# Attention scores in two packed passes of 128 rows and a third of 32 rows on two row groups

## Chip, core and metric

One core of a Trainium2 chip runs the whole kernel. The metric is the device time of one execution in microseconds (us). TensorE (PE) multiplies, VectorE (DVE), ScalarE (ACT) and GpSimd (POOL) work on the results, and SyncE (SP) issues most DMAs.

## What is computed

Two layers of a decoder trunk over 528 tokens (16 learned "meta" tokens and 512 others) with 1024 channels. Each layer projects the normed input, mixes one part by causal pooling and another by latent attention, gates both and adds them to the residual. The change is in the scores of the attention; 8 heads, each with 64 plain and 32 rotary dimensions:

```python
q = (c_q @ w_q_b).reshape(B, L, N_HEADS, QK_HEAD_DIM)          # 64 + 32
k = jnp.concatenate([k_nope, k_pe], axis=-1)                   # k_pe shared by the heads
q, k = rmsnorm(q, g_qn), rmsnorm(k, g_kn)                      # then rotary on the last 32
s = jnp.einsum('bqhd,bkhd->bhqk', q[:, q0:kend], k[:, :kend]) * scale
s = jnp.where(valid, s, MASK_VALUE); p = softmax(s); o = p @ v
```

## The kernel before

**Precision.** Every operand of a product is split into a rounded high part (type float32r) and a low part, the rest. A product is three matmuls into the same PSUM bank: high by high, high by low, low by high (`mm3`, L210 to L214; the big projections go through it as L211, L212, L213). A matmul has a stationary operand, loaded by a weight load of 128 columns, and a moving one.

**Scores of a head** (`head`, L825). Rows of the operands are the 96 dimensions. `qh` and `ql` (tiles `qhl`) hold the high and low part of the queries, `kh` and `kl` those of the keys. Even heads use 96 rows: 64 plain ones, then 32 rotary ones; odd heads 128, with the rotary ones at 0 and zeros at 32 to 63. For block i of 128 queries the moving operand is the keys up to its end: 144, 272, 400 and 528 columns. The last is cut at column 240 (`SPL`) into 240 and 288. So a head has five score pieces, of 272 (`s1`), 240 (`s3`), 400 (`s2`), 288 (`s4`) and 144 (`s0`) columns, three passes each; in layer 0 a sixth of 16 queries by 16 keys (`sm_`, the meta tokens). They lie in three PSUM banks, all of the pool `S` with three buffers: `sa` holds `s1` and `s3`, `sb` holds `s2`, `sc` holds `s4`, `s0` and `sm_`. `scores` (L838) writes the large pieces, `passes` (L890) those of 144 and 16 columns, which the profile shows as L891. `top` (L842, on DVE) adds the mask and takes the row's extreme, `expo` (L849, on ACT) takes the exponential (L850), and `turn` (L852) transposes on DVE and copies the meta columns on POOL.

**Operands of a head** (`prep`, L803). ACT rounds 64 rows of queries (L811), DVE takes their rest (L814), POOL copies the rotary rows of keys (L819) and queries (L821) and, for even heads, 64 rows of keys (L817). `prep` of head h + 1 is called behind `head` of head h. `rope_keys` (L566) makes the rotary keys of four heads at a time, `keys` (L795) the plain ones of two.

**What sets the order.** The program is written as a stream of projections (`stream`, L220) between whose steps the attention of a layer is laid by hand: `gap` (L1159) and `fill_now` (L303) advance the stream by so many nominal ns. On top of that a scheduler orders the instructions of every engine by the dependences and its own estimates. `follow` (L312) fixes an order between two instructions without a wait, `behind` (L316) adds a wait. On each engine instructions run in the order that results.

**Other places.** `qk_stats` (L764) takes the norms of queries and keys: `stat_go` (L530) sums squares with small matmuls (L538), `stat_rows` (L542) copies them with ACT (L546) into `srows`, a tile zeroed at the start (L163). `kr_sums` (L504) and `norm_sums` (L430) are matmuls too whose stationary operand is 32 columns wide at column positions 0, 32, 64 and 96; L538 has 16 columns at such positions. `pv` (L976) multiplies by the values with stationary operands of 128 columns (L994) and 64 (L997).

Of the kernel before, what the change touches and what calls it, by code (L numbers as in the profile page):

```python
# [43 lines left out]

C_ID, C_MASK = 0, 128
C_IK, C_IR = 256, 286
C_KPE, C_CQ = 306, 314
C_MM, C_VBD, C_INVF, C_CNT = 330, 346, 354, 355
N_CONST = 419

# [31 lines left out]
def trunk(ctx, tc, xT, xrow, mrow, pos, win, wkr, wqb, wkb, wvb, wgr, wpu, wmu, wout, gains, const, yT):  # L82
# [69 lines left out]
    posb = slot("u3", I32)  # L152
    ident = cst[:, C_ID:C_ID + P]
    ones = cp.tile([P, P], F32, name="ones")
# [6 lines left out]

    srows = cp.tile([32, T], F32, name="srows")
    gp.memset(srows, 0.0)  # L163

# [138 lines left out]
    def fill_now(ns):  # L303
        end = clk[0] + ns
        while clk[0] < end and step():
            pass
# [47 lines left out]
    class Layer:  # L354
# [187 lines left out]
        def stat_rows(self):  # L542
            t, n = srows, 2 * H
# [17 lines left out]
        def spread_rope(self, r):  # L561
            self.bcr = bc = slot("bc", bufs=3)
            for i in range(4):
                sp.dma_start(bc[32 * i:32 * i + 32], kdr[self.l][4 * r + i:4 * r + i + 1, :].partition_broadcast(32))

# [198 lines left out]
        def qk_stats(self):  # L764
            fill_now(LAG + 700)
            self.stat_go()
            self.stat_rows()
            sts = srows
            fill_now(2600)
# [33 lines left out]
        def prep(self, h):  # L803
            p, odd = h // 2, h % 2
            n0, r0 = (64, 0) if odd else (0, 64)
            kd = self.ks[p][odd]
            g0, gq = 32 * (h % 4), 32 * SEAT[h % 4]
            qh, ql = qhl[odd]
            x0 = self.x0
            src = self.qn[p][n0:n0 + 64, x0:T]  # L810
            made = act.activation(qh[n0:n0 + 64, x0:T], src, AF.Copy)  # L811
            if h == 0:
                behind(made, newest[0])
            dve.tensor_sub(ql[n0:n0 + 64, x0:T], src, qh[n0:n0 + 64, x0:T].bitcast(F32))  # L814
            if odd == 0:
                for d, f in zip(kd, self.ks[p][1]):
                    gp.tensor_copy(d[0:64, :], f[0:64, :])  # L817
            for d, f in zip(kd, self.kr[h // 4]):
                gp.tensor_copy(d[r0:r0 + 32, :], f[g0:g0 + 32, :])  # L819
            for d, f in zip((qh, ql), self.qr[h // 4]):  # L820
                gp.tensor_copy(d[r0:r0 + 32, x0:T], f[gq:gq + 32, x0:T])  # L821
            m = P if odd else QK
            return [t[0:m] for t in (*kd, qh, ql)]

        def head(self, h, kq, prev):  # L825
            kh, kl, qh, ql = kq
            odd = h % 2
# [9 lines left out]

            def scores(i, out, a, b):  # L838
                q0 = NM + P * i
                return mm3(out, qh[:, q0:q0 + P], ql[:, q0:q0 + P], kh[:, a:b], kl[:, a:b], True, True)  # L840

# [23 lines left out]
            top(1, 1, s1, causal(272))  # L865
            top(3, 4, s3, maskw[:, 0:SPL])
            sb = sct()
            s2 = sb[:, 0:400]
            scores(2, s2, 0, 400)
            top(2, 2, s2, causal(400))  # L870
# [14 lines left out]
            self.gap()  # L885
            sc = sct()
            s0, s4 = sc[:, 0:144], sc[:, 144:144 + T - SPL]
            scores(3, s4, SPL, T)

            def passes(out, q0, n):  # L890
                return [lambda k=k, q=q, x=x: pe.matmul(out, q[:, q0], x[:, 0:n], start=k == 0, stop=k == 2)  # L891
                        for k, (q, x) in enumerate(((qh, kh), (qh, kl), (ql, kh)))]

            todo = passes(s0, slice(NM, NM + P), 144)
            if not self.last:
                sm_ = sc[0:NM, 432:432 + NM]
                todo += passes(sm_, slice(0, NM), NM)
            for fn in todo:
                fn()
            if not self.last:  # L900
# [117 lines left out]
        def meta_queries(self):  # L1018
# [9 lines left out]
            dve.tensor_mul(smeta, smeta, bc(mxm))  # L1028
            tr = sm.tile([32, P], F32, tag="smt", name=nm("smt"))
            dve.transpose(tr, self.smeta32.rearrange("p a b -> p (a b)"))  # L1030
# [210 lines left out]
def constants():  # L1241
    c = np.zeros((P, N_CONST), np.float32)
    r = np.arange(P)
    c[:, C_ID:C_ID + P] = np.eye(P)
    c[:, C_MASK:C_MASK + P] = np.where(r[None, :] <= r[:, None], 0.0, NEG)
# [62 lines left out]
```

## Time and profile before

| | us |
|---|---|
| median of 3 runs | 754.3 (754.03 to 754.93) |
| profiled execution | 755.48 |
| its span in the trace | 753.7 |
| TensorE busy in the span | 748.1 |

A row of the order in time has a start, a duration, the engine (PE for matmuls, PEld for weight loads), the line, the operands (out<-in), the stationary tile as rows*columns and the moving operand as rows x columns. Matmuls are pipelined, so their durations overlap: what a matmul holds TensorE for is read from one start to the next. A row of the waits has who waited for whom, the us in total, the times and the longest. A row of a stretch has its length, then each engine's busy us with its count of instructions, the granted TensorE clock, the DMA share and GB/s.

### The profile page before, as it was taken

What the parts mean: (1) busy time and instruction counts of PE and PEld (TensorE: products, weight loads), DVE (VectorE), ACT (ScalarE), POOL (GpSimd) and SP (SyncE); (2) the same over time, 40 slices, a digit from 0 to 9 for tenths busy, and PEclk for the clock granted to TensorE, in tenths of its full rate; (3) what the DMA queues carried; (4) which work ended last, traced back from release to release, by engine and by line L of the source; (5) the groups of instructions that cost most, each with busy time, mean ns of one, the idle gap of its engine ahead of it and who ended that gap; (6) DMA issues with size and microseconds to landing.
All of it is one profiled execution on the core that took longest, in us unless ns stands there. A gap on an engine that the chain in (4) does not pass through costs nothing.

```text
span 753.7 us, 14317 instructions
## 1 busy us (share of the span) xinstructions
PE 748.1 (99%) x5010; PEld 681.9 (90%) x5010; DVE 562.3 (75%) x1214; ACT 395.2 (52%) x864; POOL 241.8 (32%) x294
## 2 busy tenths in 40 slices
PE   9999999999999999999999999999999999999998
PEld 9999899999999999999997898887788888887887
DVE  5588777658999987694367478678589999966942
ACT  6755656554656555543254456455445665554321
POOL 2126404704552520161130264038043526102400
PEclk9999999999999999999999999999999999999999
DMA  8633223434766576425643332233356666763462
GB/s 280 179 103 118 70 81 91 112 96 142 206 163 177 170 202 176 129 91 165 183 135 91 108 113 73 82 91 107 105 151 216 181 175 189 203 167 98 129 223 87
DMA packets 72798, 106.55 MB, mean 141 GB/s; under 512 B 14051, under 2 KB 34915, under 8 KB 72726
## 3 DMA queue, kind: packets, MB, share of 16 engines
q1 hardware_dynamic: 72582, 105.38, 47.8%
q8 instruction: 39, 0.64, 0.4%
q14 instruction: 33, 0.27, 0.1%
q10 hardware_dynamic: 144, 0.26, 0.1%
HBM read 89.76 MB, written 15.85 MB: 140 GB/s over the span
## 4 chain that ended last, share of the span: by engine, by line
PE 94%; DMA 4%; SPq 1%; DVE 1%; ACT 0%; issue 0%; ACTq 0%; DVEq 0%
PE mm L211 28%; PE mm L213 28%; PE mm L212 28%; PE S L211 2%; PE S L213 2%; PE S L212 2%; DMA raw<-wmu 1%; PE o L994 1%; DMA rdr<-rs 1%; PE o L997 1%; PE S L891 1%; PE S L538 1%; PE S L504 0%; DMA raw<-win 0%; DMA cq<-rdr 0%; DMA xb<-xT 0%
## 5 line engine op out<-in xcount | busy, mean ns | idle before, releaser
L213 PE MATMUL mm<-hh,wlo 128*128 128x264 f32 (+2 forms) x1072 | 337.0, 316 | 0.0
L212 PE MATMUL mm<-hl,whi 128*128 128x264 f32 (+2 forms) x1072 | 336.4, 315 | 0.0
L211 PE MATMUL mm<-hh,whi 128*128 128x264 f32 (+2 forms) x1072 | 336.3, 315 | 0.0
L207 DVE TENSOR_TENSOR wlo<-raw,whi 128x512 fp32r<-128x512 f32 (+2 forms) x239 | 179.6, 754 | 87.5 <-ACT whi L206 83.9
L206 ACT ACTIVATE whi<-raw 128x512 fp32r<-128x512 f32 (+2 forms) x239 | 143.0, 600 | 167.3 <-PE mm L212 133.2
L211 PEld LDWEIGHTS mm<-hh,whi 128*128 128x128 f32 x1072 | 201.4, 188 | 14.1 <-DVE vt L704 0.8
L212 PEld LDWEIGHTS mm<-hl,whi 128*128 128x128 f32 x1072 | 201.6, 188 | 13.0
L213 PEld LDWEIGHTS mm<-hh,wlo 128*128 128x128 f32 x1072 | 200.9, 188 | 12.3
L652 POOL TENSOR_TENSOR racc<-racc,tmp 128x264 f32<-128x264 f32 (+1 forms) x15 | 14.9, 993 | 117.7 <-ACT tmp L651 117.7
L1069 POOL TENSOR_TENSOR tmp<-tmp,xb 128x264 f32<-128x264 f32 (+1 forms) x24 | 27.7, 1166 | 41.8 <-DVE tmp L1067 39.7
L821 POOL CAST qhl<-q 32x528 fp32r<-32x528 f32 (+1 forms) x32 | 27.6, 876 | 40.5 <-PE S L891 39.1
L843 DVE CUSTOM_DVE_ANT_0 S<-S,maskw,nqs 128x240 f32<-128x240 f32 (+4 forms) x80 | 37.9, 493 | 1.5 <-PE S L213 1.3
L211 PE MATMUL mm<-cq,whi 128*128 128x264 f32 (+1 forms) x108 | 34.7, 321 | 0.0
L212 PE MATMUL mm<-th,whi 128*128 128x264 f32 (+1 forms) x108 | 34.6, 321 | 0.0
L213 PE MATMUL mm<-u,wlo 128*128 128x264 f32 (+1 forms) x108 | 34.5, 320 | 0.0
L212 PE MATMUL mm<-cq,whi 128*128 128x264 f32 (+1 forms) x108 | 34.5, 321 | 0.0
L213 PE MATMUL mm<-cq,wlo 128*128 128x264 f32 (+1 forms) x108 | 34.5, 321 | 0.0
L211 PE MATMUL mm<-u,whi 128*128 128x264 f32 (+1 forms) x108 | 34.5, 319 | 0.0
L938 POOL TENSOR_TENSOR u<-u,cq 128x512 f32<-128x512 f32 x8 | 12.9, 1616 | 64.6 <-DMA cq<-rdr 41.2
L853 POOL COPY pm<-cq 128x16 f32<-128x16 f32 x32 | 17.9, 559 | 44.4 <-ACT cq L850 42.3
L850 ACT ACTIVATE cq<-S,bia 128x400 f32<-128x400 f32 (+2 forms) x48 | 24.4, 512 | 13.9 <-DVE bia L904 12.8
L973 DVE TENSOR_TENSOR attE<-attE,th 128x640 fp32r<-128x640 f32 x32 | 25.6, 828 | 6.1 <-ACT th L972 6.1
(305 smaller groups left out, 1401.2 us busy)
## 6 DMA issues: line engine op xcount, KB each, us to landing
raw<-win SPq DMA_DIRECT2D x143, 256.0 KB, 3.5
pdr<-attD SPq DMA_DIRECT2D x16, 640.0 KB, 3.6
attE<-pdr SPq DMA_DIRECT2D x64, 160.0 KB, 3.6
raw<-wout SPq DMA_DIRECT2D x32, 256.0 KB, 3.0
raw<-wpu SPq DMA_DIRECT2D x16, 256.0 KB, 2.7
raw<-wmu SPq DMA_DIRECT2D x16, 256.0 KB, 2.7
raw<-wqb SPq DMA_DIRECT2D x12, 256.0 KB, 2.6
xb<-xT SPq DMA_DIRECT2D x8, 264.0 KB, 5.6
```

What stands on the lines that cost most here:

```text
L206: act.activation(hi[:, :n], raw[:, :n], AF.Copy)
L207: dve.tensor_sub(lo[:, :n], raw[:, :n], hi[:, :n].bitcast(F32))
L211: first = pe.matmul(out, wh, xh, start=start, stop=False)
L212: pe.matmul(out, wh, xl, start=False, stop=False)
L213: newest[0] = pe.matmul(out, wl, xh, start=False, stop=stop)
L652: self.acc_last = gp.tensor_add(self.acc[:, a:b], self.acc[:, a:b], t[:, :b - a])
L821: gp.tensor_copy(d[r0:r0 + 32, x0:T], f[gq:gq + 32, x0:T])
L843: return dve.tensor_tensor_reduce(out=sv, in0=sv, in1=mask, scale=nqs[:, i, h:h + 1], scalar=3e38, op0=ALU.add, op1=ALU.min, accum_out=bia ...
L850: act.activation(pv, sv, AF.Exp, scale=-1.0, bias=bia[:, i:i + 1], accum_out=rs[:, c:c + 1])
L853: gp.tensor_copy(pm[:, i, 16 * odd:16 * odd + 16], pt[i][:, 0:NM])
L973: dve.tensor_sub(got[:, a:b], f[:, a:b], hi[:, a:b].bitcast(F32))
L1069: gp.tensor_add(t[:, :b - a], t[:, :b - a], self.am[m][:, a:b])
```

## The change

The 96 dimensions times three products are 288 rows. They are packed into two passes of 128 rows and a third of 32:

- pass one: the plain key's high part stands in rows 0 to 63 and again in 64 to 127 (`both`), against the query's low part in one half and its rounded part in the other (`one`);
- pass two: the plain key's low part, the rotary key's high and its low part (`rest`), against the plain query's high part and twice the rotary query's high part (`two`);
- third pass: the rotary query's low part by the rotary key's high part, 32 rows.

The third pass has three forms ("lanes"). `pad` uses 128 rows of `low`, zero but for 32, and stays a pass over the whole array: that of `s1`. `side` takes the 32 rows of `low` and `rest` at row 64 or 0, `seat` those of the rotary tiles at their seat, row 0, 64, 32 or 96; both give the matmul a position in the rows of the array (`tile_position`). `side` serves `s2` and `s3`, `seat` serves `s4`, `s0` and `sm_`, so that neighbours in the source write to different banks. These four or five third passes are written in one burst, ordered by `follow`, early in the head; `sc` is therefore taken at its start, and the first passes of `s2`, `s4`, `s0`, `sm_` start from what the burst wrote.

`prep` has, per head, two more ACT copies and one POOL copy more. The row tile of the statistics is no longer zeroed once at the start: `qk_stats` takes the slot `cq9` for it and zeroes it there on POOL. Two tiles `qlow` are zeroed at the start in place of four strips of `qhl` and `srows`. An unused identity leaves the constants (419 to 271 columns), a tile of `meta_queries` becomes a temporary, and `spread_rope` seats the rotary keys as the queries are.

```diff
-        for j in range(2):
-            gp.memset(qhl[0][j][96:128, :].bitcast(F32), 0.0)
-            gp.memset(qhl[1][j][32:64, :].bitcast(F32), 0.0)
+    qlow = [cp.tile([P, T], F32R, name=f"qlow{i}") for i in range(2)]
+    for t in qlow:
+        gp.memset(t.bitcast(F32), 0.0)
...
         def qk_stats(self):
             fill_now(LAG + 700)
+            self.srows = slot("cq9")[0:32, 0:T]
+            gp.memset(self.srows, 0.0)
             self.stat_go()
             self.stat_rows()
...
-            made = act.activation(qh[n0:n0 + 64, x0:T], src, AF.Copy)
+            made = act.activation(two[n0:n0 + 64, x0:T], src, AF.Copy)
...
-            dve.tensor_sub(ql[n0:n0 + 64, x0:T], src, qh[n0:n0 + 64, x0:T].bitcast(F32))
+            dve.tensor_sub(one[n0:n0 + 64, x0:T], src, two[n0:n0 + 64, x0:T].bitcast(F32))
+            act.activation(one[r0:r0 + 64, x0:T], src, AF.Copy)
             if odd == 0:
-                for d, f in zip(kd, self.ks[p][1]):
-                    gp.tensor_copy(d[0:64, :], f[0:64, :])
-            for d, f in zip(kd, self.kr[h // 4]):
-                gp.tensor_copy(d[r0:r0 + 32, :], f[g0:g0 + 32, :])
-            for d, f in zip((qh, ql), self.qr[h // 4]):
-                gp.tensor_copy(d[r0:r0 + 32, x0:T], f[gq:gq + 32, x0:T])
-            m = P if odd else QK
-            return [t[0:m] for t in (*kd, qh, ql)]
+                fb, fr = self.ks[p][1]
+                gp.tensor_copy(rest[0:64, :], fr[0:64, :])
+                gp.tensor_copy(both[0:64, :], fb[0:64, :])
+                act.activation(both[64:128, :], fb[0:64, :].bitcast(F32), AF.Copy)
+            else:
+                act.activation(both[0:64, :], both[64:128, :].bitcast(F32), AF.Copy)
+            krh, krl = (t[g:g + 32, :] for t in self.kr[h // 4])
+            qrh, qrl = (t[g:g + 32, :] for t in self.qr[h // 4])
+            gp.tensor_copy(rest[r0:r0 + 32, :], krh)
+            gp.tensor_copy(rest[y0:y0 + 32, :], krl)
+            gp.tensor_copy(two[r0:r0 + 32, x0:T], qrh[:, x0:T])
+            gp.tensor_copy(two[y0:y0 + 32, x0:T], qrh[:, x0:T])
+            gp.tensor_copy(low[r0:r0 + 32, 144:T], qrl[:, 144:T])
+            return (both, rest, one, two), (low, rest, None), (qrl, krh, g), (low[r0:r0 + 32, :], rest[r0:r0 + 32, :], r0)
...
+            def scores(i, out, a, b, start, stop):
+                q = cols(i)
+                first = pe.matmul(out, one[:, q], both[:, a:b], start=start, stop=False, skip_group_check=True)
+                newest[0] = pe.matmul(out, two[:, q], rest[:, a:b], start=False, stop=stop, skip_group_check=True)
+                return first
+
+            def third(i, out, a, b, lane, start, stop):
+                w, x, r = lane
+                kw = {} if r is None else dict(tile_position=(r, 0))
+                return pe.matmul(out, w[:, cols(i)], x[:, a:b], start=start, stop=stop, skip_group_check=True, **kw)
...
-            scores(1, s1, 0, 272)
-            scores(3, s3, 0, SPL)
+            scores(1, s1, 0, 272, True, False)
+            was = third(1, s1, 0, 272, pad, False, True)
+            follow(scores(3, s3, 0, SPL, False, False), was)
             top(1, 1, s1, causal(272))
+            sb, sc = sct(), sct()
...
+            burst = [lambda: third(2, s2, 0, 400, side, True, False), lambda: third(3, s4, SPL, T, seat, True, False),
+                     lambda: third(3, s3, 0, SPL, side, False, True), lambda: third(0, s0, 0, 144, seat, False, False)]
+            if not self.last:
+                burst.append(lambda: third(-1, sm_, 0, NM, seat, False, False))
+            ins = None
+            for fn in burst:
+                was, ins = ins, fn()
+                if was is not None:
+                    follow(ins, was)
             top(3, 4, s3, maskw[:, 0:SPL])
-            scores(2, s2, 0, 400)
+            scores(2, s2, 0, 400, False, True)
...
-            sc = sct()
-            scores(3, s4, SPL, T)
...
+            scores(3, s4, SPL, T, False, True)
+            scores(0, s0, 0, 144, False, True)
```

What the scheduler makes of it on TensorE. First head 0 of layer 0 before (line, matmul, out<-moving,stationary; tiles with their numbers, moving shape; `mm` rows are projections):

```order
L213 MATMUL S_2531<-kh_2476,qhl_108 128x240
L212 MATMUL S_2540<-kl_2477,qhl_107 128x400
L213 MATMUL S_2540<-kh_2476,qhl_108 128x400
L212 MATMUL S_2626<-kl_2477,qhl_107 128x288
L213 MATMUL S_2626<-kh_2476,qhl_108 128x288
L891 MATMUL S_2626<-kh_2476,qhl_107 128x144
L891 MATMUL S_2626<-kl_2477,qhl_107 128x144
L891 MATMUL S_2626<-kh_2476,qhl_108 128x144
L891 MATMUL S_2626<-kh_2476,qhl_107 16x16
L891 MATMUL S_2626<-kl_2477,qhl_107 16x16
L891 MATMUL S_2626<-kh_2476,qhl_108 16x16
```

The same head in the changed kernel, at two places: L855 is the third pass (`qlow` with `kl` is a side, `q` with `cq` a seat), L848 pass one, L849 pass two; L207 to L209 are the lines of `mm3`.

```order
L208 MATMUL mm_2669<-hl_7_145,whi_2596 128x264
L855 MATMUL S_2541<-kl_2477,qlow_109 128x400
L855 MATMUL S_2542<-cq_420_2470,q_317_1813 128x288
L848 MATMUL S_2541<-kh_2476,qhl_105 128x400
L209 MATMUL mm_2669<-hh_6_144,wlo_2597 128x264
```

```order
L207 MATMUL mm_2771<-hh_10_148,whi_2696 128x264
L855 MATMUL S_2534<-kl_2477,qlow_109 128x240
L855 MATMUL S_2542<-cq_420_2470,q_317_1813 128x144
L855 MATMUL S_2542<-cq_420_2470,q_317_1813 16x16
L848 MATMUL S_2542<-kh_2476,qhl_105 128x288
L849 MATMUL S_2542<-kl_2477,qhl_106 128x288
L848 MATMUL S_2542<-kh_2476,qhl_105 128x144
```

The burst of one head has become two pieces, 60 rows apart, each between passes over the whole array. In head 3 of layer 0, in the changed kernel, the 400 and the 288 stand each for itself:

```order
L207 MATMUL mm_3240<-hh_6_144,whi_3166 128x264
L855 MATMUL S_3205<-kl_2810,qlow_110 128x400
L848 MATMUL S_3205<-kh_2809,qhl_107 128x400
L849 MATMUL S_3205<-kl_2810,qhl_108 128x400
L208 MATMUL mm_3240<-hl_7_145,whi_3166 128x264
```

```order
L207 MATMUL mm_3240<-hh_10_148,whi_3166 128x264
L855 MATMUL S_3206<-cq_420_2470,q_317_1813 128x288
L208 MATMUL mm_3240<-hl_11_149,whi_3166 128x264
L209 MATMUL mm_3240<-hh_10_148,wlo_3167 128x264
L207 MATMUL mm_3239<-hh_12_150,whi_3235 128x264
```

Here the third passes fill three pieces: 400; 288; and, eleven rows on, 240 with 144 and 16. Over the 16 heads there are 40 such pieces.

More of the change, by code (lines that the diff above doesn't have):

```diff
@@ L542, in stat_rows @@
         def stat_rows(self):
-            t, n = srows, 2 * H
+            t, n = self.srows, 2 * H
             for s, (a, b) in enumerate(FULL):
@@ L885, in head @@
             self.gap()
-            sc = sct()
-            s0, s4 = sc[:, 0:144], sc[:, 144:144 + T - SPL]
-            scores(3, s4, SPL, T)
[L890 to L894, printed above, removed]
+            scores(3, s4, SPL, T, False, True)
+            scores(0, s0, 0, 144, False, True)
             if not self.last:
[L896 to L899, printed above, removed]
+                scores(-1, sm_, 0, NM, False, True)
             if not self.last:
@@ L1028, in meta_queries @@
             dve.tensor_mul(smeta, smeta, bc(mxm))
-            tr = sm.tile([32, P], F32, tag="smt", name=nm("smt"))
+            tr = tmp()[0:32, 0:P]
             dve.transpose(tr, self.smeta32.rearrange("p a b -> p (a b)"))
```

35 lines of the change are left out of this document (15 added, 20 removed).

## Prediction

> **What bounds the kernel now.** I read the page's busy times and the shares of its chain first, then TensorE's waits, then the busy times of the two stretches of attention (165 to 300 us in layer 0, 545 to 660 us in layer 1), and last the order in time of TensorE's records.
>
> ```profile
> PE 748.1 (99%) x5010; PEld 681.9 (90%) x5010; DVE 562.3 (75%) x1214; ACT 395.2 (52%) x864; POOL 241.8 (32%) x294
> PE 94%; DMA 4%; SPq 1%; DVE 1%; ACT 0%; issue 0%; ACTq 0%; DVEq 0%
> ```
> ```profile
> PE mm L211 <- DVE cq L1058: 1.1, 1, 1.1
> PE wps L158 <- DVE na L774: 1.1, 1, 1.1
> PE S L994 <- ACT th L972: 0.2, 1, 0.2
> ```
> ```profile
> 165.00:300.00 135.00, 135.00 (x1096) 133.86 (x1095) 121.55 (x321) 79.82 (x203) 48.52 (x71) 1.00 0.61 174
> 545.00:660.00 115.00, 115.00 (x563) 96.57 (x561) 107.31 (x249) 67.41 (x157) 46.70 (x69) 1.00 0.64 185
> ```
>
> TensorE is busy for the whole of both stretches (135.00 of 135.00 us, 115.00 of 115.00), it waits for 2.4 us in the whole run, and the clock is 1.00. So whatever the score products lose or gain on TensorE comes out at the end one for one, and whatever the other engines do costs nothing until TensorE waits for it. The sum is made against the profiled execution (755.48 us, span 753.7), and the difference is then put on the median, 754.3, which is 1.2 us lower.
>
> **What a score pass costs now.** The end of head 0 of layer 0, from TensorE's records; the columns are start, duration, engine, line, operands, stationary tile, moving shape:
>
> ```profile
> 180.24 0.28 PE L213 MATMUL S<-kh,qhl 96*128 96x240 f32 x1
> 180.36 0.35 PE L212 MATMUL S<-kl,qhl 96*128 96x400 f32 x1
> 180.54 0.34 PE L213 MATMUL S<-kh,qhl 96*128 96x400 f32 x1
> 180.72 0.29 PE L212 MATMUL S<-kl,qhl 96*128 96x288 f32 x1
> 180.86 0.29 PE L213 MATMUL S<-kh,qhl 96*128 96x288 f32 x1
> 180.99 0.23 PE L891 MATMUL S<-kh,qhl 96*128 96x144 f32 x1
> ...
> 181.33 0.17 PE L891 MATMUL S<-kh,qhl 96*16 96x16 f32 x1
> 181.36 0.37 PE L213 MATMUL mm<-hh,wlo 128*128 128x264 f32 x1
> ```
>
> Durations overlap, so I read starts. A pass of 400 columns holds TensorE 0.18 us (0.45 ns a column), one of 288 about 0.135, one of 240 about 0.115. The six passes of L891 (three of 144 columns, three of 16) take 0.37, so 0.12 for one of each. That is more than 160 columns at 0.45 ns (0.07), because of the weight loads:
>
> ```profile
> 293.54 0.53 PEld L1042 LDWEIGHTS mm<-mh,vb 96*128 96x128 f32 x4
> 219.07 0.19 PEld L212 LDWEIGHTS S<-kl,qhl 128*128 128x128 f32 x1
> 180.86 0.19 PEld L891 LDWEIGHTS S<-kh,qhl 96*128 96x128 f32 x1
> ```
>
> Four loads of 128 columns take 0.53 us, one alone 0.19, so one follows another after (0.53 - 0.19) / 3 = 0.11 us, and 96 rows load no faster than 128. A load normally lies under the matmul ahead of it; a matmul under 0.11 us cannot cover one.
>
> **The change on TensorE.** The number of instructions stays: per head 15 passes with loads of 128 columns, in layer 0 three more of 16. Full passes over 128 rows cost what those over 96 and 128 do now. The third pass of 272 columns stays a full one. So 11 of the 15 cost what they did: 0. What changes is the four or five passes of 32 rows. If their two row groups ran at once and nothing else happened, the shorter lane would vanish. But in the order shown above they do not stand together: between them the scheduler has put full passes. I counted the runs of neighbouring 32-row passes ("pieces") over all 16 heads: **40 pieces** where the source writes 16 bursts. 12 are the 400 alone, 8 the 288 alone, 4 hold 400 and 288, 12 hold 240 and 144 (six with the 16), 4 hold 288, 240 and 144 (two with the 16). 20 of the 40 have nothing to overlap with, and each is entered from full passes and left to them.
>
> What entering and leaving costs is not in the trace for row groups. The nearest rows are the bursts on column groups (L430, L504):
>
> ```profile
> 25.94 0.28 PE L212 MATMUL mm<-hl,whi 128*128 128x264 f32 x1
> 26.06 0.28 PE L213 MATMUL mm<-hh,wlo 128*128 128x264 f32 x1
> 26.27 0.11 PEld L430 LDWEIGHTS mm<-q,ones 128*32 128x32 f32 x2
> 26.27 0.42 PE L430 MATMUL mm<-q,ones 128*32 128x264 f32 x2
> ...
> 26.53 2.16 PE L504 MATMUL S<-xb,kn 128*32 128x264 f32 x30
> ```
> ```profile
> 27.86 0.84 PE L504 MATMUL S<-xb,kn 128*32 128x264 f32 x8
> 28.62 0.19 PEld L211 LDWEIGHTS mm<-hh,whi 128*128 128x128 f32 x1 [0.42 <-issue]
> 28.62 0.39 PE L211 MATMUL mm<-hh,whi 128*128 128x264 f32 x1
> 28.73 0.19 PEld L212 LDWEIGHTS mm<-hl,whi 128*128 128x128 f32 x1
> 28.85 0.28 PE L212 MATMUL mm<-hl,whi 128*128 128x264 f32 x1
> ```
>
> In: 0.21 us from 26.06 to 26.27, where a pass of 264 takes 0.12, so 0.09 lost, and the first load starts no earlier than its matmul. Between: 30 records at (2.16 - 0.39) / 29 = 0.061, so each of four lanes takes 0.24 a record: lanes do run at once. Out: the last record starts at 27.86 + 0.84 - 0.39 = 28.31 and has streamed by 28.55; the next load starts at 28.62, 0.07 later, and lies open: 0.23 to the next matmul in place of 0.12, 0.11 lost. The same two switches with a 128-column load at both sides cost 0.09 + 0.11 + 0.07 + 0.11 = **0.38 us a piece**. The other bound is zero, by these rows, where a stationary of 64 columns alternates with one of 128:
>
> ```profile
> 209.48 0.40 PE L997 MATMUL o<-attE,vt 128*64 128x512 f32 x1
> 209.71 0.34 PE L994 MATMUL o<-th,vt 128*128 128x384 f32 x1
> 209.89 0.34 PE L997 MATMUL o<-attE,vt 128*64 128x384 f32 x1
> 210.07 0.28 PE L994 MATMUL o<-th,vt 128*128 128x256 f32 x1
> 210.19 0.28 PE L997 MATMUL o<-attE,vt 128*64 128x256 f32 x1
> ```
>
> 0.23, 0.18, 0.18, 0.12: nothing is lost there. The new passes are like the first in that they stand at positions of their own and unlike in their type (the column bursts read plain float32, two records each). I take 0.38, since position is what the change alters.
>
> The Trainium skill, TensorEngine Tiling (Array Packing), Key Properties, says that a change of tiling mode, not of tile alone, drains TensorE. By that rule each piece pays; the column bursts agree (0.09 and 0.07), the rows of 64 and 128 columns do not. The same skill, TensorE: Matmul & The Clock Gate, section The mechanism (Part 3), has loads and matmuls of different row groups overlap; by that alone the change would gain, and no run here shows it for row groups.
>
> Overlap inside the pieces, with loads 0.11 apart: 400 and 288 take 0.11 + 0.135 = 0.245 in place of 0.315, 0.07 saved, 4 times; 240 and 144 about 0.20 in place of 0.24, 0.04 saved, 12 times; 288, 240 and 144 0.31 in place of 0.37, 0.06 saved, 4 times. Sum 1.0 us.
>
> **Sum:** 40 x 0.38 - 1.0 = 15.2 - 1.0 = +14.2 us: span 767.9, the profiled execution 769.7, the median **768.5**.
>
> **The rest of the change**, at nothing:
>
> ```profile
> L821 POOL CAST qhl<-q 32x528 fp32r<-32x528 f32 (+1 forms) x32 | 27.6, 876 | 40.5 <-PE S L891 39.1
> L811 ACT ACTIVATE qhl<-q 64x528 fp32r<-64x528 f32 x8 | 5.1, 640 | 2.8 <-PE S L891 2.8
> 186.24 0.38 ACT L850 ACTIVATE pa<-S,bia 128x144 f32<-128x144 f32 x1
> 149.18 2.35 PE S L538 x40
> 1.12 0.53 POOL L163 MEMSET srows<- 32x528 f32 x1
> ```
>
> One more POOL copy a head (0.88 us) and two more ACT copies (0.64 each) lie on engines that are busy 95 and 147 of 250 us in attention, under TensorE's gemm. The memset of the rows now waits for the last reader of `cq9`; POOL's copies for head 0 queue behind it and ACT's two row copies wait for it: 0.53 us, under the 2.35 us of the statistics matmuls that ACT waits for anyway. The shorter constants stand behind the loads that layer 0 begins with. If that cover is gone, each us of lateness is a us of TensorE.
>
> **Rivals.** (1) The switch drains but loads run ahead of it: 0.09 + 0.07 = 0.16 a piece, 6.4 us, less 0.4 of overlap: 760.3. For it: in full passes loads do run ahead; against: they don't at the column bursts. (2) Switching is free and TensorE ends earlier, the other side. Price: if only loads limit (0.11 each), a piece of 400 and 288 takes 0.22 in place of 0.315, 4 times, the others nothing: -0.4 us. If the shorter lane vanishes: 4 x 0.135 + 12 x 0.10 + 4 x 0.115 = -2.2 us. So 752.1 to 753.9, 753.2 as its time; it decides once a piece costs under some 0.02 us more than it hides. For it: the rows of 64 and 128 columns; against: the column bursts, and half of the pieces being alone. (3) Switching is free, but TensorE waits for a score bank: the 32-row pass of 288 writes early in the head into the bank that the exponential of 144 columns of the head before reads last. That one ended at 186.62, 5.3 us behind the last score pass (181.33); in the new order 48 rows of some 0.12 us, 5.9 us, lie between in heads 0 and 1. It decides once that chain grows by over 0.6 us, and two ACT copies ahead of it are 1.3. With 0.7 us at three or four of the heads: 756.5. (4) The passes don't run at once at all: that takes the 1.0 us off the forecast's overlap, 769.5, inside its range.
>
> **Chances.** Drain with open loads (with 4): 0.46, own range 764 to 771.5. Rival 1: 0.20. Rival 2: 0.27. Rival 3: 0.07. About 0.2% (1.5 us) is what a measurement of this kernel can tell from no change. Slower by over that: 0.46 + 0.20 + 0.07 = 0.73. Rival 2 splits at 752.8: faster 0.13, same 0.14. The range has to reach into rival 2 and leaves out the lowest of it and a forecast made worse by waits: 752.6 to 771.5.
>
> **What would show it.** Right: the first 32-row pass of a piece starts about 0.09 us later than columns allow, its load starts with it, and the first full pass behind a piece is followed after about 0.11 us more than its columns take; the two stretches of attention grow by some 14 us together, and TensorE's waits stay near 2.4 us. Wrong: loads of 32 rows start under the full pass ahead (rival 1 or 2), pieces cost less than 0.1 us each, or TensorE's waits for ACT on `S` grow (rival 3). A 32-row load far under 0.11 us, which nothing here shows, would cut the forecast by up to 40 x 0.11 = 4.4 us.

## The result: 774.8 us, and the profile after

The changed kernel takes 774.83 us (median of 4 runs, 773.34 to 775.85), the kernel before 754.61 beside it: ratio 1.0267, 95% interval 1.0247 to 1.0287. Slower, as forecast, but by 20.2 us and not by 14.2, and outside the range. The profiled execution is the fastest of the four (773.34, span 771.5): 17.8 us of span are seen in the trace. The other 2.4 us lie in which runs were profiled: the profiled execution before (755.48) is 0.9 us above its median, the one after 1.5 us below its own, and no trace shows where the longer runs of the change lose those 1.5 us.

The page's busy times and the shares of its chain:

```profile
PE 764.3 (99%) x5010; PEld 682.3 (88%) x5010; DVE 560.3 (73%) x1214; ACT 416.6 (54%) x896; POOL 247.8 (32%) x309
PE 94%; DMA 3%; DVE 1%; SPq 1%; issue 0%; ACT 0%; ACTq 0%
```

TensorE's waits:

```profile
PE S L1011 <- ACT th L989: 2.6, 1, 2.6
PE wps L156 <- DVE na L772: 1.1, 1, 1.1
PE mm L1026 <- DMA racc<-mdr: 0.4, 2, 0.2
```

The two stretches of attention, and the end; then the end in the kernel before:

```profile
165.00:300.00 135.00, 135.00 (x1045) 128.19 (x1045) 118.98 (x309) 87.39 (x209) 49.25 (x77) 1.00 0.58 172
545.00:660.00 115.00, 114.82 (x524) 89.48 (x523) 95.43 (x216) 70.75 (x154) 46.74 (x68) 1.00 0.58 165
660.00:771.50 111.50, 105.59 (x484) 85.20 (x482) 66.66 (x119) 41.39 (x80) 17.88 (x18) 0.96 0.48 145
```
```profile
660.00:753.70 93.70, 89.43 (x417) 73.22 (x415) 53.70 (x77) 32.60 (x58) 14.60 (x11) 1.00 0.48 141
```

TensorE is still busy all through attention, but 1045 and 524 matmuls fit where 1096 and 563 did: each piece takes longer. Behind 660 us there is something else: the mean clock falls from 1.00 to 0.96, and TensorE stands idle for 5.9 us (105.59 busy of 111.50) in place of 4.3.

**First part: the pieces.** A pass of 400 columns that stands alone, in order of time:

```profile
191.57 0.28 PE L209 MATMUL mm<-hh,wlo 128*128 128x264 f32 x1
191.69 0.28 PE L207 MATMUL mm<-hh,whi 128*128 128x264 f32 x1
191.91 0.45 PE L855 MATMUL S<-kl,qlow 32*128 32x400 f32 x1
192.28 0.45 PE L848 MATMUL S<-kh,qhl 128*128 128x400 f32 x1
192.57 0.34 PE L849 MATMUL S<-kl,qhl 128*128 128x400 f32 x1
```

Read by starts: 264 columns take 0.22 us where 0.12 is their due; the 400 columns of 32 rows take 0.37, due 0.18; the 400 columns behind them 0.29, due 0.18. Together 0.40 by these rounded starts, 0.39 by the exact ones. A piece of two lanes, matmuls and then weight loads:

```profile
177.74 0.28 PE L208 MATMUL mm<-hl,whi 128*128 128x264 f32 x1
177.95 0.45 PE L855 MATMUL S<-kl,qlow 32*128 32x400 f32 x1
177.95 0.40 PE L855 MATMUL S<-cq,q 32*128 32x288 f32 x1
178.33 0.45 PE L848 MATMUL S<-kh,qhl 128*128 128x400 f32 x1
178.62 0.28 PE L209 MATMUL mm<-hh,wlo 128*128 128x264 f32 x1
```
```profile
177.95 0.18 PEld L855 LDWEIGHTS S<-kl,qlow 32*128 32x128 f32 x1
177.95 0.18 PEld L855 LDWEIGHTS S<-cq,q 32*128 32x128 f32 x1
178.33 0.19 PEld L848 LDWEIGHTS S<-kh,qhl 128*128 128x128 f32 x1 [0.19 <-issue]
```

Both lanes load and start at once, so the 288 columns cost nothing: 0.26 us over the columns of all the passes. From the exact starts of all the records, with a pass that is shorter than its weight load counted at the 0.11 us of the load: the 20 single pieces cost 0.38 to 0.40 each (one has a wait of 0.2 beside it), pairs and longer ones 0.21 to 0.28, and **the 40 pieces 13.0 us** together, of 17.8.

**Second part: the last head of layer 1.** Before, its last score pass, ACT's rounding of its transposed weights (`th`), and TensorE at the product with the values that needs it, which does not wait:

```profile
654.27 0.28 PE L891 MATMUL S<-kh,qhl 128*128 128x144 f32 x1
673.37 1.37 ACT L972 ACTIVATE th<-attE 128x640 fp32r<-128x640 f32 x2 [2.70 <-DMA attE<-pdr]
675.90 0.40 PE L994 MATMUL S<-th,vt 128*128 128x512 f32 x1
```

The same in the changed kernel, with what follows:

```profile
674.28 0.28 PE L849 MATMUL S<-kl,qhl 128*128 128x144 f32 x1
694.43 1.36 ACT L989 ACTIVATE th<-attE 128x640 fp32r<-128x640 f32 x2 [4.90 <-DMA attE<-pdr]
```
```profile
692.89 0.39 PE L209 MATMUL mm<-hh,wlo 128*128 128x512 f32 x1
695.85 0.80 PE L1011 MATMUL S<-th,vt 128*128 128x512 f32 x1 [2.56 <-ACT th L989]
696.44 0.63 PE L207 MATMUL mm<-hh,whi 128*128 128x512 f32 x1
696.87 0.63 PE L208 MATMUL mm<-hl,whi 128*128 128x512 f32 x1
...
702.65 0.39 PE L207 MATMUL mm<-q,whi 128*128 128x512 f32 x1
702.88 0.39 PE L208 MATMUL mm<-kn,whi 128*128 128x512 f32 x1
```

TensorE waits 2.56 us, and then passes of 512 columns start 0.43 us apart in place of 0.23 until about 702; the granted clock from 695.40 to 702.10 is 0.50. Work that took 6.6 us would have taken 3.3 at the old pace and with a further wait of 0.2: some 3 us lost to the clock. With the waits (4.1 in all in place of 2.4) that is the other 4.8 us.

### The profile page after: what moved, and what is told of

Its sections match the earlier page's. It is cut to its first block, busy times and chain, and to the rows that moved or that the text cites. A ratio compares the mean times of both kernels' runs of the same rounds, so it can differ in the third digit from the quotient of the medians.

```text
span 771.5 us, 14394 instructions
## 1 busy us (share of the span) xinstructions
PE 764.3 (99%) x5010; PEld 682.3 (88%) x5010; DVE 560.3 (73%) x1214; ACT 416.6 (54%) x896; POOL 247.8 (32%) x309
## 4 chain that ended last, share of the span: by engine, by line
PE 94%; DMA 3%; DVE 1%; SPq 1%; issue 0%; ACT 0%; ACTq 0%
PE mm L209 28%; PE mm L207 28%; PE mm L208 27%; PE S L848 2%; PE S L855 2%; PE S L849 1%; PE o L1011 1%; PE S L207 1%; PE o L1014 1%; PE S L209 1%; PE S L208 1%; PE S L534 1%; DMA racc<-mdr 1%; DMA pdr<-attD 1%; PE wps L156 1%; DMA mdr<-cq 1%
## 5 line engine op out<-in xcount | busy, mean ns | idle before, releaser
L209 PE MATMUL mm<-hh,wlo 128*128 128x264 f32 (+2 forms) x1072 | 337.6, 317 | 0.0
L207 PE MATMUL mm<-hh,whi 128*128 128x264 f32 (+2 forms) x1072 | 336.6, 315 | 0.0
L207 PEld LDWEIGHTS mm<-hh,whi 128*128 128x128 f32 x1072 | 201.6, 189 | 14.3 <-DVE vt L700 0.8
L209 PEld LDWEIGHTS mm<-hh,wlo 128*128 128x128 f32 x1072 | 201.2, 188 | 12.6
L858 DVE CUSTOM_DVE_ANT_0 S<-S,maskw,nqs 128x272 f32<-128x272 f32 (+4 forms) x80 | 38.6, 495 | 10.6 <-PE S L849 7.3
L868 POOL COPY pm<-cq 128x16 f32<-128x16 f32 x32 | 15.2, 476 | 74.6 <-ACT cq L865 74.1
L207 PE MATMUL mm<-cq,whi 128*128 128x264 f32 (+1 forms) x108 | 34.7, 321 | 0.0
L209 PE MATMUL mm<-u,wlo 128*128 128x264 f32 (+1 forms) x108 | 34.7, 321 | 0.0
L209 PE MATMUL mm<-cq,wlo 128*128 128x264 f32 (+1 forms) x108 | 34.5, 321 | 0.0
L207 PE MATMUL mm<-u,whi 128*128 128x264 f32 (+1 forms) x108 | 34.5, 319 | 0.0
L989 ACT ACTIVATE th<-attE 128x640 fp32r<-128x640 f32 x32 | 21.8, 730 | 16.7 <-PE S L849 8.5
```

The lines of the kernel that those rows point to most:

```text
L207: first = pe.matmul(out, wh, xh, start=start, stop=False)
L209: newest[0] = pe.matmul(out, wl, xh, start=False, stop=stop)
L858: return dve.tensor_tensor_reduce(out=sv, in0=sv, in1=mask, scale=nqs[:, i, h:h + 1], scalar=3e38, op0=ALU.add, op1=ALU.min, accum_out=bia ...
L989: behind(act.activation(hi[:, a:b], f[:, a:b], AF.Copy), newest[0])
```

## The experiments

**Theory 1 at first:** the 40 pieces cost what the forecast said, and the rest is the late last head, whose cause was first sought in the place of its products with the values. **Rivals:** the new preparation and order cost time by themselves; the wait only moves; the price hangs on position or type and not on the rows of a tile. "Cover" below is TensorE's work between the last score pass of layer 1 and the first product with the values of that head: by the starts 654.27 to 675.90 before (21.6 us), 674.28 to 695.85 less the wait of 2.56 after (19.0).

### All third passes over the whole array

```diff
-            gp.tensor_copy(low[r0:r0 + 32, 144:T], qrl[:, 144:T])
-            return (both, rest, one, two), (low, rest, None), (qrl, krh, g), (low[r0:r0 + 32, :], rest[r0:r0 + 32, :], r0)
+            gp.tensor_copy(low[r0:r0 + 32, x0:T], qrl[:, x0:T])
+            return (both, rest, one, two), (low, rest, None), (low, rest, None), (low, rest, None)
```

The products of layer 1's last head are also held behind the third group of the first output tile (`follow(held[0], newest[0])` in `stream`).

> The changed kernel with all third passes over the whole array (the 32 rows among zeros, no positions), and the product of values of layer 1's last head held behind the matmuls of mu1 so that it doesn't stand at the head of TensorE's queue too early. Theory 1 (what costs is each passage between 32-row passes and passes over the whole array, 0.25 to 0.39 us, 13.0 us in all, and 4.8 us more at the last head of layer 1): no such passages, so 753 to 757 us. Rival A (the new preparation and the order the scheduler made of it cost the time, not the row groups): 768 to 775 us, since both stay. Rival B (packing two passes into 128 full rows costs something by itself): between them, with steps of the L848 and L849 passes longer than 0.45 ns a column.

791.75 us, ratio 1.0491 (1.0471 to 1.0510). No piece is left, yet it is the slower kernel:

```profile
PE mm L1031 <- DMA racc<-mdr: 12.6, 4, 6.0
PE mm L207 <- DVE tmp L664: 3.6, 2, 2.6
PE mm L207 <- DVE tmp L1034: 2.9, 1, 2.9
```

All of TensorE's waits sum to 24.8 us, and a mean clock of 0.983 over 789.5 us takes some 13 us more; less the 2.4 us of waits before, that is all of the 35.8 us by which the span is longer. Theory 1 fails here: without any short pass, preparation and order alone make these waits, so they are no term of zero. Rival A had the cause, but its range ended 17 us too low. Rival B falls: a packed pass of 400 columns takes 0.18 us, as a pass of 400 did before.

### The products of the last head held back

The change with that one order edge alone.

```diff
-                chain(pe.matmul(o[:, P * j:512], vt[:, j, h, :], hi, start=j == 0, stop=j == 3))
+                made = chain(pe.matmul(o[:, P * j:512], vt[:, j, h, :], hi, start=j == 0, stop=j == 3))
+                if j == 0 and h == H - 1 and self.last:
+                    held.append(made)
...
+                        if g_.name == (DEPTH - 1, "mu1") and k == 2:
+                            follow(held[0], newest[0])
```

> The changed kernel with one more order edge: the first product of values of layer 1's last head stands behind the third K tile of mu1, about 5 us later in TensorE's queue. Theory 1 says that TensorE's wait of 2.6 us there, and the slow clock after it, cost 4.8 us beside the 13.0 us of the pieces: 768 to 770 us, no wait over 1 us there, clock 1.00 in the last stretch, and the 40 pieces as before at 13.0 us. Rival (the wait only moves to the next product that needs the last head, since the DMA of its blocks is what is late): 773 to 775 us.

775.20 us, 1.0281 (1.0263 to 1.0298). The wait for `th` is gone and another has come:

```profile
PE mm L1031 <- DMA racc<-mdr: 4.1, 1, 4.1
```

The rival was right, 0.2 us above its range. More cover for the products alone does not help, because what else follows the late scores is late too: here the last load of `racc`, which SP issues at 695.43, behind the transfers of the last head, and the clock falls again (0.996 over the run).

### The burst kept whole by force

The change with order edges that let nothing stand inside a burst, the preparation of the next head moved ahead, the first head of a layer set back by nominally 2.6 us, and the edge above. `ahead` are the passes written before the burst; `near` does the same for those written behind it.

```diff
-                kq = self.prep(h + 1)
+                kq = self.ready
...
+            ahead = hist[-NEAR:]
             for fn in burst:
                 was, ins = ins, fn()
-                if was is not None:
-                    follow(ins, was)
+                for other in ahead if was is None else [was]:
+                    follow(ins, other)
+            tail[:] = ins, NEAR
```

> The changed kernel with each head's burst kept whole: order edges put the 120 matmuls traced before it ahead and the 120 after it behind, the next head's operands are prepared before the second half of the head, and the product of values of the last head is held as in the run beside it. 16 pieces of five (layer 0) or four passes in place of 40. Theory 1: a piece costs 0.38 us less what the shorter lane hides (288, 144 and 16 beside 400 and 240: about 0.27), so 0.1 to 0.2 us each, 2 to 3 us in all: 755 to 759 us where TensorE doesn't wait, and more by exactly the waits the trace shows for prepared operands, since the burst can no longer move. Rival C (a 32-row pass is slow by itself, whatever stands beside it): the 72 passes cost their 13 us as before, 767 us or more without waits.

814.05 us, 1.0789 (1.0753 to 1.0826): 16 pieces, and the largest wait is

```profile
PE S L869 <- DVE bia L872: 27.0, 15, 5.1
```

The short pass of `s3` waits inside the burst for `top(1)`, since `s1` and `s3` share the bank `sa` and `top(1)` is written ahead of the burst. So a burst kept whole has a wait inside; split, with full passes between, it covers that wait and pays for one more passage. Theory 1 was wrong on the price of waits: they sum to 35.0 us, but the span is 61 longer than before's, because the clock, 0.966 on average, takes another 27.

### What a change of tile costs, by itself

The kernel before with one extra pass of 256 columns, in six forms, ahead of the accumulations of two gemms (`gp`, `gm`). It overwrites nothing that is used, and adds work.

```diff
+        if form == 0:
+            pe.matmul(ps[:, 0:256], w[:, 0:P], x, start=True, stop=True)
+        elif form == 1:
+            pe.matmul(ps[:, 0:256], w[32:64, 0:P], x[32:64], start=True, stop=True, tile_position=(32, 0))
+        elif form == 2:
+            pe.matmul(ps[:, 0:256], w[0:32, 0:P], x[0:32], start=True, stop=True)
...
+        elif form == 4:
+            pe.matmul(ps[:, 0:256], w[64:128, 0:P], x[64:128], start=True, stop=True, tile_position=(64, 0))
```

> The kernel before, with one extra matmul of 256 moving columns ahead of each accumulation of gp and gm, into the bank that the accumulation then overwrites (the output stays the same). Six forms in turn: 0 whole array; 1 32 rows at row 32; 2 32 rows at row 0 without a position; 3 32 columns at column 32, plain float32; 4 64 rows at row 64; 5 whole array, plain float32. Price of a form: the steps around it less what 256 columns take (0.117 us; twice two records for float32). Theory 1 (the shape of the tile decides): 0 costs 0; 1, 2 and 4 each 0.38; 3 about 0.27 (its load has 32 columns); 5 costs 0. Rival D (the position decides, not the size): 2 costs 0. Rival E (the type made the column bursts dear): 5 costs as much as 3.

One execution: 773.22 us, clock 1.00. The form with 64 rows:

```profile
230.31 0.28 PE L213 MATMUL mm<-hh,wlo 128*128 128x264 f32 x1
230.52 0.38 PE L230 MATMUL mm<-hh,whi 64*128 64x256 f32 x1
230.84 0.39 PE L211 MATMUL mm<-hh,whi 128*128 128x264 f32 x1
231.06 0.29 PE L212 MATMUL mm<-hl,whi 128*128 128x264 f32 x1
```

0.21, 0.32 and 0.22 us for columns worth 0.12, 0.12 and 0.12: 0.39 lost. Over all probes, by exact starts: 32 rows at row 32 0.39, 32 rows at row 0 without a position 0.39, 64 rows at row 64 0.39, 128 rows under 0.01, but for one behind a pass of 144 columns. Plain float32 over the whole array took 0.43 to 0.47 a pass for its two records, whether one stood alone or two together, so it paid no switch. The 32 columns at column 32, also in float32, cost about 0.3 more than that. So among tiles of fewer rows it is the number of rows that costs, not the position, which the prediction had taken, and not the type. For tiles of fewer columns this is open: 32 at column 32 paid, 64 at column 0 (in the prediction's rows) did not, and no run moved the one or the other.

The Trainium skill, TensorEngine Tiling (Array Packing), Key Properties, has a change of mode drain TensorE. These rows agree and give the price; the full passes of 96 rows among those of 128 (in the prediction's rows) don't pay it.

### The old order with the new packing

The change with each third pass over the whole array right behind its own two, and `sc` taken in the second half as before.

```diff
-            sb, sc = sct(), sct()
+            sb = sct()
...
+            def block3(i, out, a, b):
+                first = scores(i, out, a, b, True, False)
+                newest[0] = third(i, out, a, b, pad, False, True)
+                return first
```

**Theory 1 from here on:** the longer preparation makes the scheduler put the last head's scores later in TensorE's stream, and that is what is late. **Rival:** the bank `sc`, held through the whole head.

> The change's packing and its preparation (ACT, POOL copies), with every third pass over the whole array (its short operand padded with zeros) right behind its own two packed passes, and with the kernel before's order: bank sc taken only in the second half of a head. No short passes, so no pieces: what is over 754.4 is the preparation and the order it gives. Theory 1 (the preparation, above all POOL's longer share, lets the scheduler put the last head's scores of layer 1 later, 651.0 us of TensorE's work in place of 645.1, 19.2 us of cover in place of 21.8): the wait and the slow clock at that place return, 756.5 to 761. Rival (bank sc held through the whole head and the burst between the halves make the waits): 753 to 755.5.

762.59 us, 1.0113 (1.0091 to 1.0135). The rival falls: the old order of the banks does not bring 754 back. Theory 1 is right only in part: its range ended 1.6 us too low, the wait for `th` is back at the last head, but the slow clock is not (1.00 from 684 to 700 us). Most of the loss lies elsewhere: all waits sum to 6.9 us in place of 2.4, the clock falls once in layer 0 (0.50 from 263.80 to 267.10), and of the 8.8 us of span some 2.5 are in neither. The largest waits:

```profile
PE S L1008 <- ACT th L986: 1.5, 1, 1.5
PE mm L207 <- DVE tmp L1026: 1.3, 1, 1.3
```

### Bank sc held early, in the kernel before

```diff
-            sb = sct()
+            sb, sc = sct(), sct()
             s2 = sb[:, 0:400]
+            s0, s4 = sc[:, 0:144], sc[:, 144:144 + T - SPL]
+            scores(3, s4, SPL, T)
             scores(2, s2, 0, 400)
```

> The kernel before with one part of the change alone: bank sc is taken in the first half and the 288-column block of s3 is scored ahead of s2, so that sc is held through the head. Rival (holding the bank makes the waits): 756 to 761, with TensorE's waits named by exp or gate of sc. Theory 1: the cover stays 21.5 us and nothing moves, 753.5 to 755.5.

755.59 us, 1.0021 (1.0006 to 1.0036), 0.1 us over theory 1's range and below the rival's. Holding the bank costs 0.06 to 0.36 per cent, and no wait names the exponential.

### top(1) behind the burst

```diff
             follow(scores(3, s3, 0, SPL, False, False), was)
-            top(1, 1, s1, causal(272))
             sb, sc = sct(), sct()
...
+            top(1, 1, s1, causal(272))
             top(3, 4, s3, maskw[:, 0:SPL])
```

> The change with one line moved: top(1) on VectorE stands behind the burst, not ahead of it, so that the 240-column third pass in the same bank need not wait for it. 31 pieces in place of 40, and the last head's scores are back at 645.6 us of TensorE's work with 23.2 us of cover. Theory 1: 31 pieces by 0.33 us (13.0 us for 40) = 10.1, and the wait at the last head is gone: 763.5 to 766.5. Rival (the cost goes by short passes, not by pieces): 13 us as before, 767 to 769.5. Rival (top(1) late makes exp late, new waits for bank sa): over 770.

763.29 us (763.06 to 763.70), 1.0121 (1.0106 to 1.0136), 0.2 us under theory 1's range. One moved line takes back 11.5 of the 20.2 us. All of TensorE's waits, and the end:

```profile
PE wps L156 <- DVE na L772: 1.1, 1, 1.1
```
```profile
660.00:761.90 101.90, 98.76 (x466) 80.98 (x464) 62.75 (x102) 36.75 (x67) 20.03 (x18) 1.00 0.48 150
```

The 31 pieces cost 8.7 us by their starts, against a span 8.2 longer than before's, whose TensorE waits 1.3 us more: all but some 0.8 us of the difference is in the pieces. The last scores stand early again (cover 23), and wait and slow clock are gone together. The preparation here is that of the change, POOL copy included: it does not make the last head late by itself, but through the order that comes out.

### More preparation, in the kernel before

First two ACT copies and one POOL copy more per head that change no value, then the POOL copy alone:

```diff
+            gp.tensor_copy(qh[r0:r0 + 32, x0:T], self.qr[h // 4][0][gq:gq + 32, x0:T])
```

> The kernel before with two more ACT copies of 64 rows and one more POOL copy of 32 rows by 528 a head, none of which changes a value: part of the change's longer preparation, nothing of its passes. By its order the last head's scores stand at 649.5 us of TensorE's work, cover 20.8 us in place of 21.8. Theory 1: 755.5 to 759, with a wait near the last head of layer 1 over the 1.3 us of the kernel before. Rival (the preparation lies wholly beside TensorE's work): 753.8 to 755.2.

758.65 us (756.57 to 759.60), 1.0055 (1.0034 to 1.0077), inside theory 1's range. But its trace, of the fastest of the four runs, does not have the wait near the last head: the cover there is 20.9 us, `th` is ready just as TensorE comes to it, and the clock is 1.00. Where the slower runs lose their time was not traced.

> The kernel before with one more POOL copy of 32 rows by 528 a head that changes no value, and nothing on ACT. Its order puts the last head's scores at 647.2 us of TensorE's work, cover 18.5 us. Theory 1 (the order that a longer preparation on POOL brings is what costs): 756 to 760, most of the 4.6 us that the run with this copy and two ACT copies lost. Rival (the two ACT copies were the cause): 753.8 to 755.

758.55 us (757.10 to 761.06), 1.0067 (1.0046 to 1.0087). One copy of 0.9 us a head, on an engine with most of its time free, costs what all three do; the ACT copies add nothing that can be measured. This trace, unlike the one before it, has the wait and the slow clock. The last head's products, with that copy alone:

```profile
675.12 0.40 PE L211 MATMUL mm<-hh,whi 128*128 128x512 f32 x1
677.76 0.64 PE L997 MATMUL S<-th,vt 128*128 128x512 f32 x1 [2.24 <-ACT th L975]
678.20 0.63 PE L212 MATMUL mm<-hl,whi 128*128 128x512 f32 x1
678.62 0.63 PE L213 MATMUL mm<-hh,wlo 128*128 128x512 f32 x1
```

It is the picture of the changed kernel: a wait for `th`, then steps of 0.43 us (clock 0.50 from 677.98 to 681.38). From its last score pass (656.94) to ACT's `th` (676.34) are 19.4 us; before they are 19.1, after 20.2. That way through DVE, a DMA out and four back hardly changes; what changes is the cover, 18.6 us here and 21.6 before.

### Whole bursts with top(1) behind them

The forced burst again, with the moved line of the run with `top(1)` behind the burst.

> The change with top(1) behind the burst, the burst of each head kept whole by order edges, the next head's preparation moved ahead of the second half and the products of layer 1's last head held back (cover 29.7 us): 16 pieces of 400, 288, 240, 144 and 16 columns. Theory 1 (what counts is the number of pieces and what the lanes hide in each; the two pieces of this kind in the run with top(1) moved cost 0.15 and 0.08 us over their columns): 16 by 0.08 to 0.15 = 1.3 to 2.4 us, 755.5 to 757. Rival (a whole burst waits in TensorE's stream for the preparation or for VectorE again): over 760, with the waits named at the passes of the burst. Rival (shorter lanes hide nothing): 16 by 0.39 = 6.2, 760 to 761.

776.17 us, 1.0302 (1.0284 to 1.0319). Theory 1 was right on the pieces and wrong on the time. A whole burst:

```profile
568.35 0.27 PE L863 MATMUL S<-kl,qhl 128*128 128x240 f32 x1
568.55 0.45 PE L869 MATMUL S<-kl,qlow 32*128 32x400 f32 x1
568.55 0.47 PE L869 MATMUL S<-cq,q 32*128 32x288 f32 x2
568.84 0.27 PE L869 MATMUL S<-kl,qlow 32*128 32x240 f32 x1
569.03 0.45 PE L862 MATMUL S<-kh,qhl 128*128 128x400 f32 x1
569.32 0.34 PE L863 MATMUL S<-kl,qhl 128*128 128x400 f32 x1
```

0.97 us from 568.35 to 569.32, for 1712 columns (240, 400, 288, 240, 144, 400). One after another these take 0.84, by 0.183 for 400, 0.132 for 288 and 0.113 for each of the three short ones, whose load is the limit: 0.14 over by the exact starts, the lanes counted as a gain already. Fourteen of the 16 bursts cost 0.10 to 0.15; of the other two, one lies in a stretch of slow clock and one has a wait inside. The time went to waits, the rival's, 12.9 us in all, and some 3 us to a slow clock behind them (0.996 on average); about 4 us of the span are in none of these. The largest:

```profile
PE o L1034 <- DVE attE L1008: 4.3, 4, 1.6
PE S L863 <- POOL kl L830: 3.5, 3, 2.5
PE S L862 <- POOL kh L831: 1.5, 1, 1.5
```

### All short passes on one row group

As with `top(1)` moved, but the third passes of `s4`, `s0` and `sm_` take the lane of `s2` and `s3`.

```diff
-            gp.tensor_copy(low[r0:r0 + 32, 144:T], qrl[:, 144:T])
-            return (both, rest, one, two), (low, rest, None), (qrl, krh, g), (low[r0:r0 + 32, :], rest[r0:r0 + 32, :], r0)
+            gp.tensor_copy(low[r0:r0 + 32, x0:T], qrl[:, x0:T])
+            return (both, rest, one, two), (low, rest, None), (low[r0:r0 + 32, :], rest[r0:r0 + 32, :], r0), (low[r0:r0 + 32, :], rest[r0:r0 + 32, :], r0)
```

> The change with top(1) behind the burst and all short passes on one row group, so that none can run beside another: 31 pieces as in the run with top(1) moved alone, cover 21.8 us. Theory 1 (the second row group hides the shorter passes, and 31 pieces cost 31 by 0.39 = 12.1 us without it in place of 8.7): 766 to 768. Rival (the lanes hide nothing that matters): 763 to 764.

768.85 us, 1.0202 (1.0187 to 1.0217). The same 31 pieces cost 11.3 us in place of 8.7, so the second row group hides 2.6 us. Of the rest of the 5.6 us between the two, 1.7 are further waits (1.4 of it for `whi`); some 1.3 were not located. Theory 1's range ended 0.9 too low. POOL's copy into `low` is also longer here, by 144 columns in layer 0 and 128 in layer 1, which may have moved the order too.

### The kernel before with the edge

The same `held` as above, in the kernel before.

> The kernel before with the products of layer 1's last head held back by one order edge, to a place behind the third pass group of the first output tile that follows: cover 31.1 us in place of 21.8. Theory 1: the kernel before already has cover enough for its own preparation and only its wait of 1.1 us goes: 752.8 to 754.3. Rival (the wait moves to what comes after the products, as it did with the change): 754.5 to 757.

754.64 us, 1.0013 (1.0003 to 1.0022): the wait of 1.1 us goes, one of 0.8 for DVE comes. This is the rival's range, not theory 1's, which ended at 754.3. No version tried beats the kernel before.

## Why the prediction came out too low

- **TensorE bounds the kernel, and what it gains or loses comes out one for one:** right within 1 us. With `top(1)` moved, 8.7 us of pieces and 1.3 us less of waits make 8.2 us of span.
- **11 of the 15 passes cost what they did:** right; pieces (13.0) and the last head (4.8) make up the 17.8 us of span, and nothing is left for them. With every pass over the whole array, one of 400 columns took the 0.18 us that it took before.
- **40 pieces by 0.38 us:** right in count and size (0.39: for a 400 alone 0.09 going in, 0.19 inside, 0.11 going out), though taken from column bursts. Rivals 1 and 2, with 0.16 and nothing, are out. Only the reason was off: position was taken to decide, and it is the rows of the tile.
- **Overlap of 1.0 us:** too small. 40 by 0.39 less the 13.0 measured is 2.6. The loads of two lanes do not stand 0.11 us apart; they start together. These two errors of size put the forecast for the pieces 1.2 us too high, 14.2 against 13.0 (1.6 by the overlap, less 0.4 by the price).
- **The rest of the change at nothing: this step failed.** The prediction priced one more POOL copy by the engine's free time, and said that TensorE's waits stay near 2.4 us. That copy alone, added to the kernel before, costs 4.9 us. It is not in the way while it runs, but the scheduler's order changes with it: the last head's scores come later among the projections, and these then end before `th` is ready (the table below). The prediction also took a us of lateness for a us of TensorE; with the slow clock behind it, it was about two. In the trace of after the last head is 4.8 of the 17.8 us; against the medians, 20.2 us apart, some 7 us are beside the pieces.
- **Rival 3, a wait for bank `sc`:** not seen. TensorE waits for ACT on `S` there, but for `th`, and holding the bank alone costs 0.2%.
- **Rival 4, lanes that don't run at once:** out; they start together, and one row group for all costs 2.6 us more in pieces.

The last head of layer 1 in the kernels above that do not hold its products back (the six forms, which add work in between, are left out), by the starts. The way is from the last score pass to the end of `th`; each row is one execution:

| kernel | cover, us | way, us | TensorE's wait for `th`, us |
|---|---|---|---|
| `top(1)` behind the burst | 23.0 | 22.4 | 0 |
| before | 21.6 | 20.5 | 0 |
| all short passes on one row group | 21.6 | 19.6 | 0 |
| before, bank `sc` held early | 21.4 | 19.2 | 0 |
| before, ACT and POOL copies added | 20.9 | 20.9 | 0 |
| the old order with the new packing | 19.2 | 20.7 | 1.5 |
| the change | 19.0 | 21.5 | 2.6 |
| before, POOL copy added | 18.6 | 20.8 | 2.2 |

TensorE waits exactly where the way is longer than the cover, and for about the difference.

Shown: the price of a piece, the overlap, that the wait is what the cover lacks of the way, and that the POOL copy, alone, was enough for the wait and the slow clock in one trace. Argued only: that in the changed kernel it is this copy rather than the other moves; there several things changed the order at once, and they were not taken apart. Against a simple rule stand three traces with the same copy and no wait: with two ACT copies beside it, with `top(1)` moved, and with one row group. Also open is why the times of some kernels differ so much between runs (754.02 to 758.85 with the bank held early, 757.10 to 761.06 with the POOL copy), while those of the kernel before, beside them, stayed within 2.3 us.

## What to carry to other kernels

A pass that uses 32 or 64 of the array's rows among passes of 96 or 128 costs 0.39 us a passage in this kernel, from full passes and back to them; a shared pass hid at most 0.13 us for 288 columns, so such a pass has to be gathered into long runs, and even a whole head's burst only comes near even (0.10 to 0.15 us lost). Count the passages in TensorE's final order, not in the source, and ask what splits a burst: here it was one mask step in the same bank. An instruction on an idle engine is free only while the order stays; where a chain through DMAs ends one phase, compare its length with the work left to cover it, because 3 us less cover cost 5 us here.

## What the chip showed beyond that

- Two matmuls on different row groups start 3 to 4 ns apart by the exact starts, with both loads at once.
- Waits of 2.24 and 2.56 us were followed by about 3.4 and 6 us in which a 512-column pass took 0.43 us in place of 0.23, at a granted clock of 0.50. So the two cost about 1.8 and 2.2 times their length. Behind the wait of 1.48 us for `th` in the old order with the new packing the clock stayed at 1.00. The Trainium skill, TensorE: Matmul & The Clock Gate, What's actually happening (Part 1), puts the fall of the clock behind an idle window of about 3.4 us. Here shorter waits were enough, and the measurement decides.
